# Pinning TensorE's instructions to program order in a two-model, single-core forward pass

## The chip, the cores and the metric

The kernel runs on one core of one Trainium2 chip. The metric is the device time of one execution in microseconds (us). Engine names are those of the profile: PE is TensorE's matrix multiply and PEld its weight load, DVE is VectorE, ACT is ScalarE, POOL is GpSimd, SP is SyncE, which issues the DMAs. Each engine works through a queue of its own, in the order in which the instructions stand there, and the queues wait for each other through semaphores.

## The reference, cut to what matters

Two blocks follow each other on a sequence of 256 positions of width 1024. All data is float32.

```python
def first_block(x, p, ...):                     # D = 1024, S = 256
    for i in range(4):                          # mixers: conv, S5 scan, RWKV7, conv
        y = mixer_i(x, ...)
        r = DN_ALPHA * x + y
        r = r + (p[i] @ ple_proj[i]) * sigmoid(r @ ple_gate[i])
        x = layer_norm(r, ln_g[i], ln_b[i])
    return x

def rwkv7_mixer(x, ...):
    ...
    w_log = -softplus(-(w0 + tanh(xw @ w1) @ w2)) - 0.5      # low-rank: 1024 -> 64 -> 1024
    a = sigmoid(a0 + (xa @ a1) @ a2)
    kk = kk / max(norm(kk), 1e-12)                            # per head of 64
    ...                                                       # recurrence over 256 positions, 16 heads

def half_ffn(h, g, shift, scale, gate, w1, w3, w2):           # 1024 -> 2816 -> 1024
    hm = rms_norm(h, g) * (1 + scale) + shift
    return h + 0.5 * gate * ((silu(hm @ w1) * (hm @ w3)) @ w2)

def second_block(x, c, ctx, c_ctx, ...):
    for l in range(2):
        mod_x, mod_c = silu(c) @ ada_w[l] + ada_b[l], silu(c_ctx) @ ada_w[l] + ada_b[l]
        x, ctx = half_ffn(x, ...), half_ffn(ctx, ...)
        hx, hc = modulated rms_norm of x and of ctx
        y_x, y_c = mixer_ab(hx, hc, ...) if l == 0 else mixer_cd(hx, hc, ...)
        x = x + mod_x[5] * y_x
        x = half_ffn(x, ...)
        if l == 0:
            ctx = half_ffn(ctx + mod_c[5] * y_c, ...)
    return x
```

`mixer_ab` is softmax attention with two kinds of heads, 8 and 8, whose queries and keys get an rms norm per head and a rotation; the tokens attend to 512 keys, their own and those of the context. `mixer_cd` has 8 heads of a chunked gated recurrence and 8 of attention in a window.

## The kernel before

**Matmuls.** Activations stand with their features on the 128 partitions, in 8 chunks of 128 features by 256 positions. A linear layer goes through tiles of weights of 128 by 1024 (8 chunks of 128 by 128). A tile `w` is brought in by a DMA on SP's queue (`get`, L590 to 605), copied into `whi` in the format fp32r by ScalarE (L601), and the rest `wlo` is formed by VectorE (L602). The activations have two halves of the same kind, so that a chunk takes three matmuls into one PSUM bank (`mm3`): hi by whi, lo by whi, hi by wlo. A tile of 8 chunks is thus 24 matmuls of 256 columns. There are four buffers each of `w`, `whi` and `wlo`, and eight PSUM banks: three for `ps_mm`, one for `ps_st`, two each for `ps_ca` and `ps_cb` (`BANKS`).

**Two orders.** The program is written by a planner while it is built. `weave` steps through two generators, the stream of the context (names with 1, as `h1_hi`) and that of the tokens (names with 0, as `d0_hi`), with a model of time of its own: a stream that yields is resumed when its operands should be ready. `par` does the same inside a stage with two or three chains, one for a head or a tile of heads. That gives out a program order for each engine. The tile framework's scheduler then orders each engine's instructions anew by its own estimate of when operands are ready; an instruction wrapped in `keep_in_program_order` can't be moved ahead of the engine's instruction before it, nor that one behind it. Before the change only a few ScalarE instructions are wrapped (table loads and the like).

**Places that the prediction speaks of.**

- `norm_mod` (entry of an FFN): sums of squares through `bsum` into `ps_st`, the root, and then for each of the eight chunks a product `tc` on VectorE, `h_hi` on ScalarE and `h_lo` on VectorE. `ffn` takes its tiles from there.
- `head_norm` (attention heads): the square `ta` of a head's values, `bsum` with a matrix of means (`second`) into a bank, `rsqrt`, and the scaling. `bsum` takes the bank `ps_st`, or a `ps_mm` where its model says that it is free earlier.
- `soft` and `attend` (softmax): scores into `ps_ca`, the maximum and the exponential, `p` times its reciprocal sum on VectorE (`p<-p,sm`), then transposes of `p` into `ps_cb` through `TensorE.transpose` (L437), and the product of the transposed `pt` with the values.
- `rates` and `heads` (RWKV): `rates` multiplies the low-rank vector by three slices of a weight, one after the other through the single bank `ps_st`, each read by a tanh on ScalarE. `heads` then works on two heads of 64 in one chain; its products of 64 by 64 go to `ps_ca` and `ps_cb`. Three chains run at a time.
- A side stream computes the modulation (`in_ada`) on VectorE alone (`junk`, L1379).

Every matmul goes through `TensorE.matmul` (L433), whose helper records the line for all of them, so that places are told apart by tiles.

Of the kernel before, what the change touches and what calls it, by code (L numbers as in the profile page):

```python
# [314 lines left out]
def free_size(ap):  # L315
    n = 1
    for d in ap.shape[1:]:
        n *= d
    return n
# [88 lines left out]
class TensorE:  # L408
# [14 lines left out]
    def matmul(self, out, lhsT, rhs, start, stop, share=1):  # L423

        n, m = free_size(rhs), out.ap[0][1]
        if rhs.dtype == F32R:
            dur = n / 2400.0
        elif m > 64 or share > 1:
            dur = max(n, 128) / 600.0 / share
        else:  # L430
            dur = 0.06 + max(n, 32) / (1200.0 if m > 32 else 2400.0)
        self.count(dur + 0.002, out, [lhsT, rhs])
        self.t.matmul(out, lhsT=lhsT, rhs=rhs, start=start, stop=stop)  # L433

    def transpose(self, out, in_, ident):
        self.count(0.11, out, [in_])
        self.t.transpose(out, in_, ident)  # L437


class Net:  # L440
# [1532 lines left out]
```

## Time and profile before

| | us |
|---|---|
| median of three runs | 2889.77 |
| lowest and highest of these | 2887.61 and 2893.28 |
| the profiled execution | 2890.76 |
| span in its trace | 2889.0 |
| busy: PE / PEld / DVE / ACT / POOL | 2749.4 / 2604.6 / 2134.0 / 1606.4 / 14.8 |
| mean granted TensorE clock, share of full | 0.977 |

The profile comes from one execution. Busy times are sums over all instructions of an engine; the idle time in brackets behind a group of instructions is what its engine stood still just before it, with what ended that. [...] A group such as "x3" in the order in time is that many instructions in a row of one shape with one set of operands.

### The profile page before, as it was taken

Reading aid. Unit: us, or ns where it says so; the run is one execution under the profiler, and the core shown is the slowest. Engines: PE = TensorE matmul, PEld = TensorE weight load, DVE = VectorE, ACT = ScalarE, POOL = GpSimd, SP = SyncE. Lnnn points to the kernel's source line nnn. Section 1 sums busy time; section 2 is a strip of 40 time slices with the busy share of each in tenths; the row PEclk is TensorE's granted clock in tenths of the full one; section 3 lists DMA queues with packets and bytes.
Section 4 is the critical chain, followed back from the end, with each engine's and each line's share of the span. In section 5 each row is a group of like instructions: output and inputs, shape, how many; then the busy total and the mean of one; then the engine's idle time right before and its main releaser. Section 6 shows DMA issues by size and latency. Waiting matters only on the chain.

```text
span 2889.0 us, 58552 instructions
## 1 busy us (share of the span) xinstructions
PE 2749.4 (95%) x23798; PEld 2604.6 (90%) x23798; DVE 2134.0 (74%) x3953; ACT 1606.4 (56%) x2976; POOL 14.8 (1%) x41
## 2 busy tenths in 40 slices
PE   8978799899999998999999999999999999999999
PEld 8967799778998998998999978999999999996999
DVE  8877777666688788899789887777855556676655
ACT  5455555766555465877666766445422234466443
POOL 0000000000000000000000000000000000000000
PEclk9989799999999999999999999999999999999999
DMA  7743355201586665666576644666543433222554
GB/s 270 238 165 110 108 167 175 82 17 40 163 269 226 220 197 167 209 215 203 182 226 195 199 130 155 203 225 194 180 142 125 139 117 103 89 82 65 161 182 139
DMA packets 132751, 467.53 MB, mean 162 GB/s; under 512 B 14720, under 2 KB 19072, under 8 KB 131840
## 3 DMA queue, kind: packets, MB, share of 16 engines
q1 hardware_dynamic: 132480, 463.78, 50.0%
q8 instruction: 187, 3.06, 0.4%
q14 instruction: 84, 0.69, 0.1%
HBM read 462.67 MB, written 1.05 MB: 161 GB/s over the span
## 4 chain that ended last, share of the span: by engine, by line
PE 72%; DVE 12%; DMA 7%; ACT 6%; issue 3%; SPq 0%; ACTq 0%; DVEq 0%
PE ps_mm L433 62%; PE ps_ca L433 5%; DMA w<-in_ada_dram 5%; DVE wlo L602 3%; PE ps_cb L433 2%; DVE junk L1379 2%; PE ps_st L433 2%; DVE ssm_m L403 2%; ACT whi L601 2%; DVE tc L403 1%; PE ps_cb L437 1%; ACT rw_b L403 1%; ACT L403 1%; ACT tc L403 1%; DMA w<-in_ab_in_dram 1%
## 5 line engine op out<-in xcount | busy, mean ns | idle before, releaser
L601 ACT ACTIVATE whi<-w 128x1024 fp32r<-128x1024 f32 (+1 forms) x687 | 715.9, 1043 | 740.2 <-PE ps_mm L433 488.1
L602 DVE TENSOR_TENSOR wlo<-w,whi 128x1024 fp32r<-128x1024 f32 (+1 forms) x687 | 825.6, 1203 | 239.2 <-ACT whi L601 236.8
L433 PE MATMUL ps_mm<-h_hi,whi 128*128 128x256 f32 x3024 | 873.1, 290 | 17.1 <-ACT h_hi L403 12.4
L433 PE MATMUL ps_mm<-h_hi,wlo 128*128 128x256 f32 x3024 | 859.5, 285 | 9.5 <-DVE wlo L602 9.5
L433 PE MATMUL ps_mm<-h_lo,whi 128*128 128x256 f32 x3024 | 856.5, 284 | 0.6 <-DVE h_lo L403 0.5
L433 PEld LDWEIGHTS ps_mm<-h_hi,whi 128*128 128x128 f32 x3024 | 573.6, 190 | 25.8 <-ACT h_hi L403 15.1
L433 PEld LDWEIGHTS ps_mm<-h_hi,wlo 128*128 128x128 f32 x3024 | 573.3, 190 | 12.2 <-DVE wlo L602 11.5
L433 PEld LDWEIGHTS ps_mm<-h_lo,whi 128*128 128x128 f32 x3024 | 577.5, 191 | 5.2 <-DVE h_lo L403 1.9
L1379 DVE SCALAR_TENSOR_TENSOR junk<-w,cond 128x1024 bf16<-128x1024 f32 x288 | 351.7, 1221 | 145.0 <-DMA w<-in_ada_dram 144.1
L433 PE MATMUL ps_mm<-d_hi,whi 128*128 128x256 f32 x1232 | 355.7, 289 | 4.1 <-DVE ctx L403 3.0
L433 PE MATMUL ps_mm<-d_hi,wlo 128*128 128x256 f32 x1232 | 350.4, 285 | 1.5 <-DVE wlo L602 1.5
L433 PE MATMUL ps_mm<-d_lo,whi 128*128 128x256 f32 x1232 | 349.2, 283 | 0.4 <-DVE d_lo L403 0.4
L433 PEld LDWEIGHTS ps_mm<-d_hi,whi 128*128 128x128 f32 x1232 | 232.3, 189 | 8.7 <-issue 5.7
L433 PEld LDWEIGHTS ps_mm<-d_lo,whi 128*128 128x128 f32 x1232 | 234.0, 190 | 3.4 <-issue 1.2
L433 PEld LDWEIGHTS ps_mm<-d_hi,wlo 128*128 128x128 f32 x1232 | 232.1, 189 | 2.8 <-DVE wlo L602 2.0
L403 DVE TENSOR_TENSOR td<-td,ps_mm 128x256 f32<-128x256 f32 x154 | 64.4, 418 | 70.0 <-PE ps_mm L433 68.9
L403 ACT ACTIVATE d_hi<-td 128x256 fp32r<-128x256 f32 x154 | 63.0, 409 | 89.5 <-DVE td L403 88.7
L403 ACT ACT_TABLE_LOAD x78 | 100.1, 1283 | 2.1 <-PEq L1964 0.7
L433 PE MATMUL ps_mm<-x_hi,whi 128*128 128x256 f32 x256 | 73.5, 287 | 12.0 <-ACT whi L601 12.0
L403 ACT ACTIVATE tc<-tc 128x256 f32<-128x256 f32 x182 | 75.1, 413 | 5.6 <-DVE tc L403 2.6
L433 PE MATMUL ps_mm<-xs_hi,whi 128*128 128x256 f32 x256 | 73.4, 288 | 4.8 <-ACT xs_hi L403 4.4
L403 ACT ACTIVATE td<-ps_mm 128x256 f32<-128x256 f32 x154 | 57.4, 374 | 32.9 <-PE ps_mm L433 32.3
(467 smaller groups left out, 5270.5 us busy)
## 6 DMA issues: line engine op xcount, KB each, us to landing
w<-in_ffn_in_dram SPq DMA_DIRECT2D x268, 512.0 KB, 4.2
w<-in_ada_dram SPq DMA_DIRECT2D x168, 512.0 KB, 4.3
w<-in_ffn_out_dram SPq DMA_DIRECT2D x96, 512.0 KB, 4.1
w<-in_conv_in_dram SPq DMA_DIRECT2D x64, 512.0 KB, 4.7
w<-in_ffn_out_dram SPq DMA_DIRECT2D x48, 384.0 KB, 3.1
w<-in_ab_in_dram SPq DMA_DIRECT2D x34, 512.0 KB, 4.4
w<-in_ple_gate_dram SPq DMA_DIRECT2D x32, 512.0 KB, 4.5
w<-in_conv_out_dram SPq DMA_DIRECT2D x16, 512.0 KB, 5.2
```

What stands on the lines that cost most here:

```text
L403: return f(**kw)
L433: self.t.matmul(out, lhsT=lhsT, rhs=rhs, start=start, stop=stop)
L437: self.t.transpose(out, in_, ident)
L601: nc.scalar.activation(out=hi[:, :n], in_=w[:, :n], func=AF.Copy)
L602: nc.vector.tensor_tensor(out=lo[:, :n], in0=w[:, :n], in1=hi[:, :n].bitcast(F32), op=ALU.subtract)
L1379: nc.vector.scalar_tensor_tensor(out=self.junk, in0=w, scalar=1.0, in1=cb[:, s], op0=ALU.mult, op1=ALU.mult, accum_out=m[:, t, s:s + 1])
```

## The change

Both calls that issue a TensorE instruction, in `matmul` and in `transpose`, are wrapped, so that TensorE's queue holds them in the order in which the planner gave them out.

```diff
@@ class TensorE
         self.count(dur + 0.002, out, [lhsT, rhs])
-        self.t.matmul(out, lhsT=lhsT, rhs=rhs, start=start, stop=stop)
+        self.net.tc.keep_in_program_order(self.t.matmul(out, lhsT=lhsT, rhs=rhs, start=start, stop=stop))
 
     def transpose(self, out, in_, ident):
         self.count(0.11, out, [in_])
-        self.t.transpose(out, in_, ident)
+        self.net.tc.keep_in_program_order(self.t.transpose(out, in_, ident))
```

Instructions and their shapes stay the same on all engines. The scheduler still orders the other engines; since it sees another TensorE, 1,056 of VectorE's instructions and some 550 of ScalarE's change place too, most by a few places, and 6 on SP by one. In the rows below, numbers behind a name tell one buffer's use from another.

TensorE before, context FFN (`h1`) beside the tokens' head norms, at the end of a tile:

```order
L433 MATMUL ps_mm_14727<-h1_hi_13309,wlo_14723 128x256
L433 MATMUL ps_mm_14727<-h1_hi_13309,whi_14722 128x256
L433 MATMUL ps_mm_14727<-h1_lo_13310,whi_14722 128x256
L433 MATMUL ps_st_14707<-ta_14661,second_12479 128x256
L433 MATMUL ps_mm_14727<-h1_hi_13309,wlo_14723 128x256
L433 MATMUL ps_mm_14773<-d0_hi_13218,whi_14768 128x256
L433 MATMUL ps_mm_14773<-d0_lo_13219,whi_14768 128x256
L433 MATMUL ps_mm_14773<-d0_hi_13218,wlo_14769 128x256
```

and in the changed program, where the same sum of squares (`ps_st_14707`) stands:

```order
L433 MATMUL ps_mm_14679<-h1_lo_13310,whi_14674 128x256
L433 MATMUL ps_mm_14679<-h1_hi_13309,wlo_14675 128x256
L433 MATMUL ps_st_14707<-ta_14661,second_12479 128x256
L433 MATMUL ps_mm_14727<-h1_hi_13309,whi_14722 128x256
L433 MATMUL ps_mm_14727<-h1_lo_13310,whi_14722 128x256
L433 MATMUL ps_mm_14727<-h1_hi_13309,wlo_14723 128x256
L433 MATMUL ps_mm_14727<-h1_hi_13309,whi_14722 128x256
```

The sum of squares stood inside the tile `ps_mm_14727`, behind 23 of its 24 matmuls; it now stands ahead of that tile.

TensorE before, at the entry of the last FFN (`h0_hi` and `h0_lo` come chunk by chunk, the three banks belong to three weight tiles):

```order
L433 MATMUL ps_st_31405<-squares_31164,cs_base_155 128x256 x2
L433 MATMUL ps_mm_31457<-h0_hi_31415,whi_31452 128x256
L433 MATMUL ps_mm_31490<-h0_hi_31415,whi_31485 128x256
L433 MATMUL ps_mm_31524<-h0_hi_31415,whi_31519 128x256
L433 MATMUL ps_mm_31457<-h0_lo_31416,whi_31452 128x256
L433 MATMUL ps_mm_31457<-h0_hi_31415,wlo_31453 128x256
L433 MATMUL ps_mm_31457<-h0_hi_31415,whi_31452 128x256
L433 MATMUL ps_mm_31490<-h0_lo_31416,whi_31485 128x256
L433 MATMUL ps_mm_31457<-h0_lo_31416,whi_31452 128x256
```

and in the changed program:

```order
L433 MATMUL ps_st_31405<-squares_31164,cs_base_155 128x256 x2
L433 MATMUL ps_mm_31457<-h0_hi_31415,whi_31452 128x256
L433 MATMUL ps_mm_31457<-h0_lo_31416,whi_31452 128x256
L433 MATMUL ps_mm_31457<-h0_hi_31415,wlo_31453 128x256
L433 MATMUL ps_mm_31457<-h0_hi_31415,whi_31452 128x256
L433 MATMUL ps_mm_31457<-h0_lo_31416,whi_31452 128x256
L433 MATMUL ps_mm_31457<-h0_hi_31415,wlo_31453 128x256
```

The three tiles were worked on side by side; now the first is finished ahead of the second, chunk by chunk.

TensorE before, in the tokens' attention beside the context's FFN (`ps_ca` are scores, `ps_cb` transposes of `p`, `d1` is the FFN):

```order
L433 MATMUL ps_mm_19998<-d1_lo_17152,whi_19993 128x256
L433 MATMUL ps_ca_19972<-kava_12481,qa_17666 128x512
L433 MATMUL ps_ca_19982<-kava_12481,qa_17666 128x512
L433 MATMUL ps_mm_19998<-d1_hi_17151,wlo_19994 128x256
L433 MATMUL ps_mm_19998<-d1_hi_17151,whi_19993 128x256
L433 MATMUL ps_mm_19998<-d1_lo_17152,whi_19993 128x256
L433 MATMUL ps_mm_19998<-d1_hi_17151,wlo_19994 128x256
L437 MATMUL ps_cb_19960<-cs_base_155,p_19902 128x128 x4
L433 MATMUL ps_mm_19998<-d1_hi_17151,whi_19993 128x256
```

and in the changed program:

```order
L433 MATMUL ps_mm_19930<-d1_hi_17151,wlo_19926 128x256
L437 MATMUL ps_cb_19960<-cs_base_155,p_19902 128x128 x4
L437 MATMUL ps_cb_19966<-cs_base_155,p_19902 128x128 x4
L433 MATMUL ps_ca_19972<-kava_12481,qa_17666 128x512
L433 MATMUL ps_ca_19982<-kava_12481,qa_17666 128x512
L433 MATMUL ps_mm_19998<-d1_hi_17151,whi_19993 128x256
```

The scores and the tile `ps_mm_19998` stood ahead of the transposes; now the transposes of both heads come first, behind the end of the tile `ps_mm_19930`.

## Rows read from the trace of the kernel before

**Rows 1.** The page: busy time by engine; the chain that ended last, by engine.

```profile
PE 2749.4 (95%) x23798; PEld 2604.6 (90%) x23798; DVE 2134.0 (74%) x3953; ACT 1606.4 (56%) x2976; POOL 14.8 (1%) x41
...
PE 72%; DVE 12%; DMA 7%; ACT 6%; issue 3%; SPq 0%; ACTq 0%; DVEq 0%
```

**Rows 2.** Busy by stage: from:to, length, PE, PEld, DVE, ACT, POOL; clock; DMA.

```profile
526.00:600.00 74.00, 61.85 (x1022) 50.31 (x1020) 42.92 (x105) 53.35 (x134) 1.10 (x1) 0.93 0.10 30
...
1180.00:1350.00 170.00, 165.08 (x1261) 155.62 (x1260) 153.51 (x321) 137.10 (x258) 0.00 (x0) 1.00 0.64 205
1480.00:1660.00 180.00, 176.47 (x1348) 169.66 (x1348) 163.47 (x301) 130.68 (x215) 0.00 (x0) 1.00 0.62 197
1660.00:1770.00 110.00, 108.84 (x713) 80.77 (x711) 87.58 (x201) 76.94 (x145) 0.00 (x0) 1.00 0.41 129
```

**Rows 3.** Order in time, last FFN's entry: start, length, operation [idle before <-releaser].

```profile
2689.61 1.01 PE L433 MATMUL ps_mm<-h_hi,whi 128*128 128x256 f32 x3 [3.44 <-ACT h_hi L403]
...
2694.05 0.41 PE L433 MATMUL ps_mm<-h_hi,whi 128*128 128x256 f32 x1
2694.26 0.60 PE L433 MATMUL ps_mm<-h_lo,whi 128*128 128x256 f32 x2
...
2695.16 0.89 DVE L403 SCALAR_TENSOR_TENSOR h_lo<-tc,mod,h_hi 128x256 fp32r<-128x256 f32 x2 [0.18 <-ACT h_hi L403]
...
2696.85 0.28 PE L433 MATMUL ps_mm<-h_lo,whi 128*128 128x256 f32 x1
2696.97 0.28 PE L433 MATMUL ps_mm<-h_hi,wlo 128*128 128x256 f32 x1
```

**Rows 4.** Busy by stretch, at the same entry.

```profile
2687.90:2694.70 6.80, 5.09 (x24) 5.09 (x25) 6.19 (x16) 2.81 (x7) 0.00 (x0) 0.50 0.19 70
2694.70:2700.00 5.30, 5.30 (x46) 5.30 (x46) 1.59 (x4) 2.33 (x4) 0.00 (x0) 1.00 0.00 0
```

**Rows 5.** Order in time, context FFN beside the tokens' head norms.

```profile
1244.69 0.28 PE L433 MATMUL ps_mm<-h_hi,wlo 128*128 128x256 f32 x1
...
1248.37 0.42 DVE L403 SCALAR_TENSOR_TENSOR tc<-ps_st,tc 128x256 f32<-128x256 f32 x1
...
1248.84 0.70 PE L433 MATMUL ps_st<-ta,second 128*128 128x256 f32 x2 [1.11 <-DVE tc L403]
1249.19 0.47 PE L433 MATMUL ps_mm<-h_hi,wlo 128*128 128x256 f32 x1
...
1251.70 0.42 DVE L403 SCALAR_TENSOR_TENSOR tc<-ps_st,tc 128x256 f32<-128x256 f32 x1
...
1252.36 0.59 PE L433 MATMUL ps_st<-ta,second 128*128 128x256 f32 x2
```

**Rows 6.** Order in time, the tokens' attention beside the context's FFN.

```profile
1662.99 0.28 PE L433 MATMUL ps_mm<-d_hi,whi 128*128 128x256 f32 x1
...
1664.30 1.88 PE L433 MATMUL ps_ca<-kava,qa 128*128 128x512 f32 x4
...
1665.93 0.48 DVE L403 TENSOR_SCALAR p<-p,sm 128x512 f32<-128x512 f32 x1
...
1666.98 0.48 DVE L403 TENSOR_SCALAR p<-p,sm 128x512 f32<-128x512 f32 x1
```

**Rows 7.** Order in time, TensorE alone, start of the RWKV heads.

```profile
526.71 0.59 PE L433 MATMUL ps_mm<-rw_b,cs_base 128*128 128x256 f32 x2
...
535.41 1.13 PE L433 MATMUL ps_st<-rwkv_c,ta 128*128 128x256 f32 x4
...
540.36 1.58 PE L433 MATMUL ps_ca<-rw_a 128*64 128x64 f32 x22 [2.19 <-DVE rw_a L403]
...
548.83 1.48 PE L433 MATMUL ps_cb<-rw_a 128*64 128x64 f32 x18 [3.48 <-DVE rw_a L403]
```

**Rows 8.** Order in time, TensorE alone, heads of two weight tiles.

```profile
1114.50 0.55 PE L433 MATMUL ps_mm<-d_hi,whi 128*128 128x256 f32 x1 [3.04 <-DVE ctx L403]
...
1151.34 0.38 PE L433 MATMUL ps_mm<-h_hi,whi 128*128 128x256 f32 x1 [2.03 <-ACT whi L601]
```

## The prediction, made before the changed kernel was run

> **What bounds the kernel now.** I read the page's busy table first, then its chain of waits, then busy times by stage, then the order in time at the places where the built programs differ. TensorE is busy for 2749.4 of 2889.0 us [rows 1], so at most 139.6 us of its idle time could go, and the chain that ended last lies 72% on TensorE [rows 1]. The reader is to see that this is no stage-by-stage pipeline with slack on TensorE: whatever makes TensorE stand still longer moves the end, unless a later standstill becomes shorter by as much. By stage, VectorE is close behind it: 153.51 of 170 us at 1180 to 1350 and 163.47 of 180 us at 1480 to 1660, against 87.58 of 110 us at 1660 to 1770 [rows 2]. The RWKV start (526 to 600) is the loosest stretch, with 61.85 of 74 us busy [rows 2].
>
> **What the change does to the work.** No instruction is added or removed and none changes its shape. TensorE's stream has 21,145 matmuls and transposes in both programs; 2,976 of them change place, all inside 102 short stretches, between which the two orders are the same. Inside a stretch the old order steps past an instruction whose operand is late and does something else; the new order stands at it. So the cost of a stretch is the wait at the late operand, less what the old order itself waited there. Matmul time is conserved: a 256-column matmul starts 0.12 us after the one before at the full clock (2696.85 to 2696.97) and 0.21 us at the half clock (2694.05 to 2694.26) [rows 3].
>
> For every one of the 102 stretches I took the moment at which each late operand landed in the trace (the end of the ACT or DVE row that writes it), let TensorE start where it started before, walked the new order at the spacings of the rows, and noted how much later the stretch ends. These sums assume that stretches don't affect each other and that the clock is full; one example of each kind follows, with what I keep of its sum.
>
> Stage entries (10 stretches, 28.7 us so counted). A normalisation hands its eight chunks h_hi and h_lo to the next linear layer one after another. At the last FFN, TensorE starts at 2689.61 when the first h_hi is there; the last h_lo lands at 2695.16 + 0.89 = 2696.05 [rows 3]. Before, three weight tiles are worked on at once as chunks arrive: 24 matmuls by 2694.7 at clock 0.50, then 48 more at 0.12 us, to about 2700.4 [rows 4]. In program order the first tile alone has matmuls whose operands are there; its last two can't start before 2696.05, and 48 of the other two tiles remain: 2696.2 + 5.8 = 2702.0, so 1.6 us later, where the full-clock sum said 3.5. Half of the entries stand at the half clock like this one, the others nearer to their full sum: I take 18, with 9 and 29 as bounds.
>
> Head norms (24 stretches, 27.9 us). A head's sum of squares goes into the one ps_st bank, which is free when DVE has read the head before. At 1248.37 + 0.42 = 1248.79 DVE does so, and ps_st starts at 1248.84 [rows 5]. Program order has it right behind the matmul at 1244.69 [rows 5]: a wait of about 4.0 us, where 1.11 was waited before; 23 matmuls that ran meanwhile are still to do, 23 x 0.12 = 2.8 us lost. The next ps_st needs the DVE step of 1251.70 + 0.42 = 1252.12 [rows 5]; behind the first loss TensorE gets there at 1249.2 + 24 x 0.12 = 1252.1 and waits for nothing, though counted alone it cost 2.7. So a pair costs 2.8 and not 5.5. Such neighbours, and a VectorE that catches up while TensorE stands, leave 16 of 27.9; bounds 8 and 28.
>
> Softmax transposes (24 stretches, 41.7 us). Program order puts the transposes of two heads ahead of the next two score matmuls and of a whole FFN tile. TensorE is there at 1662.99; the two p are ready at 1665.93 + 0.48 = 1666.41 and 1666.98 + 0.48 = 1667.46 [rows 6]: 3.4 us, and about 0.6 more behind the first four transposes. Before, none was waited: the scores (1664.30) and 24 FFN matmuls filled it [rows 6]. The scores now start some 4 us later, and with them the next softmax. Part of p's lateness is queueing on VectorE, which is worked off during the wait: I take 29; bounds 14 and 42.
>
> RWKV. Six low-rank products go through the one ps_st bank, three at once at the start. Before, the first head's norm (526.71) and some 5 us of other matmuls ran in between; the third product is at 535.41 [rows 7]. In program order the norm stands behind it, about 9.8 us later, and everything of the first head with it; but TensorE idled 2.19 us before 540.36 and 3.48 before 548.83 [rows 7] waiting for the vector work that this delays, and that work is also held by later queues. Between 0 (the three heads' vector work, not the norm, sets the pace) and 9.8 I take 5, the middle, since ACT and DVE have to do the same work either way. Of the 28 later stretches, 16.1 so counted, I keep 13; bounds 6 and 16.
>
> Others (15 stretches, 2.6 us): a late wlo now holds TensorE instead of the first two matmuls of the next tile, 0.24 us each, and one stretch gets 2.7 us shorter (below). I take 2.
>
> The ACT and DVE queues are reordered too, since their scheduler sees the pinned TensorE, by up to some 30 places; the DMA queue hardly. No row prices that: I keep it at 0, with the bounds of the vector-bound kinds holding it.
>
> Sum: 18 + 16 + 29 + 5 + 13 + 2 = 83 us on the profiled execution's 2890.8: 2973.8. That execution lies 1.0 above the median of 2889.8, so 2973.
>
> [...] The order in the queue matters only if a waiting matmul holds those behind it. In the trace it does: at 1248.84 ps_st had let TensorE idle 1.11 us while the next matmul (1249.19) belonged to a tile of which 23 matmuls had run, so its operands were there [rows 5]. [...]
>
> **Rivals.** (a) The waits are repaid: with TensorE standing, DVE gets through the weight splits earlier and every later vector step is ready sooner. For it: VectorE is busy 90% and 91% in two of the attention stages [rows 2], and the pair above. Against it: at the entries and at the RWKV start nothing else is left to work off. Only those would stay, 18 + 5 less some: about 2908. 12 in 100.
>
> (b) Nothing is repaid and the clock falls. Counted alone the kinds give 117, the RWKV start up to 10. A wait of 3.44 us had the clock at 0.50 until 2694.7 [rows 3, 4]; 24 matmuls there took 5.1 us instead of 2.9, 2.2 lost. Some 15 new waits of over 2 us could each do so, 33 us. Together 2890.8 + 160, near 3050; half of the clock loss, as likely, gives 3030. 20 in 100.
>
> (c) Faster: the old order looked ahead wrongly. It let TensorE stand at the head of the next tile, for a bank (3.04 us at 1114.50) or for its weights (2.03 us at 1151.34) [rows 8], while the present tile was nearly ready. Program order takes these away, 5.1 us with the two shown and up to 9 with smaller ones. It decides if the vector work keeps ahead of TensorE nearly everywhere, so that the other kinds cost less than this: 2881. The softmax rows speak against it, since p is 3.4 us late with VectorE full. 5 in 100.
>
> **How the numbers follow.** The forecast, 2973, has 62 in 100, with its own range from the lower bounds (9 + 8 + 14 + 0 + 6 = 37, so 2927) to the middle of (b) at 3015. Rivals: (a) 12, (b) 20, (c) 5, queue that reorders 1. For 8 in 10 I leave out (c), the reordering queue, the lower part of (a) and the top of (b): 2910 to 3030. A measurement of this kernel can tell about 0.2%, 5.8 us, from no change. Faster by more than that is (c) but for its weaker half: 0.04. Within it: the rest of (c), the reordering queue and the very end of (a): 0.04. Slower: 0.92.
>
> **What would show it.** TensorE's busy time should stay near 2749 us while its idle time grows from 139.6 to some 220. At the last FFN's entry the matmuls should run through one weight tile and stand for each pair of chunks; in the token attention the transposes should carry idle times of 2 to 4 us, ended by DVE's p, and the scores stand behind them; in the RWKV start three ps_st products should follow each other with nothing between. It would be wrong if the idle time ended by p and tc stays where it was although the order moved (a), if the granted clock shows many more stretches at half (b), or if ps_mm waits at tile heads vanish with no others in their place (c).

## The result, and the profile of the changed kernel

The changed kernel takes 3005.1 us (median of four, 3001.8 to 3009.3) against 2890.4 for the kernel before on the same chip: 1.0401 times as long, 95% interval 1.0389 to 1.0414. The prediction was 2973 with a range of 2910 to 3030. It lies within the range; the loss is 114.7 us where 83 were forecast.

The page's busy times answer to [rows 1], with the span and the mean granted clock, a share of full speed (0.977 before):

```profile
PE 2780.8 (93%) x23798; PEld 2623.6 (87%) x23798; DVE 2146.0 (71%) x3953; ACT 1611.7 (54%) x2976; POOL 14.8 (0%) x41
...
PE 14%; DVE 1%; ACT 1%; issue 0%; ACTq 0%
```

```profile
core 0: 3005.2 us, clock 0.963
```

TensorE's idle time is 3005.2 - 2780.8 = 224.4 us, 84.8 more than before; the prediction said "some 220". But its busy time, which was to stay near 2749, rose by 31.4 us with the same 23,798 instructions: 84.8 + 31.4 = 116.2, the whole difference of the spans. The chain of waits can't be held against that of before, since it was followed back over 16% of the span only.

The same stages by busy time, cut at the same instructions as [rows 2]:

```profile
526.00:608.20 82.20, 63.65 (x1018) 51.07 (x1018) 43.69 (x106) 54.42 (x134) 1.10 (x1) 0.85 0.09 27
1211.60:1393.40 181.80, 170.26 (x1253) 158.65 (x1254) 155.61 (x325) 136.34 (x258) 0.00 (x0) 0.97 0.60 192
1523.20:1723.60 200.40, 183.24 (x1348) 176.10 (x1348) 166.63 (x304) 132.35 (x215) 0.00 (x0) 0.96 0.57 180
1723.60:1853.40 129.80, 111.43 (x713) 83.43 (x712) 88.98 (x198) 76.50 (x145) 0.00 (x0) 0.96 0.33 105
```

The reader is to see two things in each line: it is longer by more than TensorE's busy time grew, which is idle time, and the granted clock, 1.00 in three of these stages before and 0.93 in the first, is now 0.85 to 0.97.

TensorE's instructions between the 102 stretches stand in the same order in both traces, so that one can read at every stretch how far the changed kernel has fallen behind. Grouped as in the prediction (one stretch was put to another group than ahead), with the growth between stretches given to the stretch that follows (all in us; the column of idle time counts inside the stretches alone):

| kind | stretches | kept in the sum | fell behind | of it idle inside |
|---|---|---|---|---|
| stage entries | 10 | 18 | 20.8 | 10.3 |
| head norms | 25 | 16 | 20.1 | 15.7 |
| softmax transposes | 23 | 29 | 44.4 | 30.3 |
| RWKV start | 1 | 5 | 8.0 | 6.2 |
| RWKV later | 28 | 13 | 16.1 | 17.7 |
| others | 15 | 2 | 7.1 | 6.8 |
| sum | 102 | 83 | 116.5 | 87.0 |

With idle time alone the sum was nearly met, but not kind by kind: the entries stood 8 us less than was kept for them, the RWKV mixer's later places and the others 5 us more each.

### The profile page after: what moved, and what is told of

The parts are those of the page before. It is cut to its first block, busy times and chain, and to the rows that moved or that the text cites. A ratio compares the mean times of both kernels' runs of the same rounds, so it can differ in the third digit from the quotient of the medians.

```text
span 3005.2 us, 58587 instructions
## 1 busy us (share of the span) xinstructions
PE 2780.8 (93%) x23798; PEld 2623.6 (87%) x23798; DVE 2146.0 (71%) x3953; ACT 1611.7 (54%) x2976; POOL 14.8 (0%) x41
## 5 line engine op out<-in xcount | busy, mean ns | idle before, releaser
L433 PE MATMUL ps_mm<-h_hi,whi 128*128 128x256 f32 x3024 | 887.6, 294 | 17.5 <-ACT h_hi L403 17.0
L433 PE MATMUL ps_mm<-h_lo,whi 128*128 128x256 f32 x3024 | 866.9, 287 | 8.5 <-DVE h_lo L403 7.6
L433 PEld LDWEIGHTS ps_mm<-h_hi,wlo 128*128 128x128 f32 x3024 | 581.2, 192 | 7.7 <-DVE wlo L602 7.7
L437 PE MATMUL ps_cb<-cs_base,p 128*128 128x128 f32 x256 | 44.1, 297 | 42.4 <-DVE p L403 33.9
L437 PEld LDWEIGHTS ps_cb<-cs_base,p 128*128 128x128 f32 x256 | 29.7, 149 | 57.5 <-issue 24.4
```

Of the source, the lines that this page charges most:

```text
L433: self.net.tc.keep_in_program_order(self.t.matmul(out, lhsT=lhsT, rhs=rhs, start=start, stop=stop))
L437: self.net.tc.keep_in_program_order(self.t.transpose(out, in_, ident))
```

## Experiments

**One kind of place at a time.** Four kernels pin TensorE only over ranges of its program order; in each the places of that kind stand as in the changed kernel and nearly all others as before. In the order of the table below 24, 26, 12 and 29 of the 102 stretches have the changed kernel's order, 88 different ones in all; the other 14, which fell 5.5 us behind under the whole change, are pinned in none. With the head norms pinned, 11 short stretches of the softmax stages behind came out in an order that neither program has.

```diff
 class TensorE:
+    def pin(self, ins):
+        if any(a <= self.n < b for a, b in PINNED):
+            self.net.tc.keep_in_program_order(ins)
+        self.n += 1
...
-        self.t.matmul(out, lhsT=lhsT, rhs=rhs, start=start, stop=stop)
+        self.pin(self.t.matmul(out, lhsT=lhsT, rhs=rhs, start=start, stop=stop))
```

> TensorE is pinned only in the softmax stages (context attention, tokens' attention, the last attention in windows); 23 of the changed places stand as in the changed kernel, all others but one as before. Theory: what the full change cost in these stages belongs to these places alone; between the same instructions the two traces grow apart there by 38.6 us inside the places and 5.8 between them, so 2890 + 44 = 2934 (2929 to 2940). The prediction's own term was 29 (2919). Rival (the loss comes from the whole program's new order on VectorE and ScalarE, or the stages pay each other back): well off 2934, near 2890 or above 2950.

> TensorE is pinned only in the stages of the attention heads' norms. Theory: 21.0 us inside the places less 1.0 between them, so 2890 + 20 = 2910 (2905 to 2916); the prediction's term was 16. But at the tokens' heads a later softmax may take the loss up, since the order of the attention behind is free again. Rival as for the softmax alone: near 2890, or above 2925.

> TensorE is pinned only at the ten stage entries. Theory: 24.5 us inside the places less 3.7 between, so 2890 + 21 = 2911 (2905 to 2917), of which idle time only 10 and the rest a lower clock; the prediction's term was 18, with no clock in it. Rival: the clock at the entries fell because of waits elsewhere; then only the idle time stays and the kernel takes 2900.

> TensorE is pinned only in the RWKV mixer (from the first products of rates to the end of its heads). Theory: 8.0 us at the start and 19.1 less 3.1 behind it, so 2890 + 24 = 2914 (2908 to 2920), nearly all of it idle time; the prediction's term was 18. Rival as above: near 2890.

| pinned | median us | against 2888.3 | ratio, 95% interval | idle | busy |
|---|---|---|---|---|---|
| softmax | 2937.5 | +49.2 | 1.0167 (1.0152 to 1.0182) | +33.0 | +15.0 |
| head norms | 2906.0 | +17.7 | 1.0059 (1.0042 to 1.0076) | +12.2 | +5.8 |
| entries | 2912.9 | +24.6 | 1.0080 (1.0065 to 1.0095) | +5.5 | +18.2 |
| RWKV | 2911.0 | +22.8 | 1.0079 (1.0064 to 1.0094) | +23.3 | -3.4 |

The last two columns come from the busy line of each page and the span, against 2749.4 of 2889.0 in [rows 1]: spans of 2937.0, 2907.0, 2912.7 and 2908.9 us, in the order of the table with

```profile
PE 2764.4 (94%) x23798; PEld 2611.8 (89%) x23798; DVE 2139.5 (73%) x3953; ACT 1609.4 (55%) x2976; POOL 14.8 (1%) x41
```

```profile
PE 2755.2 (95%) x23798; PEld 2610.2 (90%) x23798; DVE 2135.0 (73%) x3953; ACT 1603.9 (55%) x2976; POOL 14.8 (1%) x41
```

```profile
PE 2767.6 (95%) x23798; PEld 2616.2 (90%) x23798; DVE 2134.9 (73%) x3953; ACT 1607.9 (55%) x2976; POOL 14.8 (1%) x41
```

```profile
PE 2746.0 (94%) x23798; PEld 2600.7 (89%) x23798; DVE 2134.8 (73%) x3953; ACT 1605.8 (55%) x2976; POOL 14.8 (1%) x41
```

All four times lie in the ranges of the theory; of the entries' loss 5.5 us are idle time, where 10 were expected. The four losses add up to 114.3 us, each known to some 4 us, and the loss of the whole change is 114.7: the stages don't pay each other back, and the new order on VectorE and ScalarE elsewhere is not what costs. Inside a pinned stage the order of VectorE and ScalarE changes with TensorE's, and no run parts the two. The last columns show where each kind loses: the entries mostly in longer busy time (18.2 us, 5.5 of idle time), the RWKV mixer in idle time alone, the softmax stages in both.

Which instruction waits is read from the groups of instructions, whose last field is the idle time before the group and what ended it: the transposes of `p`, and the rotation of a head (`ps_ca<-tb,second`), before:

```profile
L437 PE MATMUL ps_cb<-cs_base,p 128*128 128x128 f32 x256 | 40.7, 278 | 3.9 <-DVE p L403 2.1 <-DVE sm L403 1.3
L433 PE MATMUL ps_ca<-tb,second 128*128 128x256 f32 x42 | 13.6, 406 | 2.5 <-DVE tb L403 2.1
L433 PE MATMUL ps_st<-ta,second 128*128 128x256 f32 x40 | 12.5, 393 | 2.0 <-DVE tc L403 1.9
```

in the changed kernel:

```profile
L437 PE MATMUL ps_cb<-cs_base,p 128*128 128x128 f32 x256 | 44.1, 297 | 42.4 <-DVE p L403 33.9 <-DVE sm L403 5.8 <-ACT d_hi L403 1.3
L433 PE MATMUL ps_ca<-tb,second 128*128 128x256 f32 x42 | 13.9, 414 | 14.3 <-DVE tb L403 14.3
L433 PE MATMUL ps_st<-ta,second 128*128 128x256 f32 x40 | 12.4, 392 | 3.9 <-DVE tc L403 3.6 <-ACT ta L403 0.2
```

with the softmax stages alone pinned, and with the head norms alone:

```profile
L445 PE MATMUL ps_cb<-cs_base,p 128*128 128x128 f32 x256 | 45.0, 300 | 42.9 <-DVE p L403 35.4 <-DVE sm L403 4.0 <-ACT whi L609 1.5
L441 PE MATMUL ps_ca<-tb,second 128*128 128x256 f32 x42 | 13.6, 406 | 2.4 <-DVE tb L403 2.0
```

```profile
L441 PE MATMUL ps_ca<-tb,second 128*128 128x256 f32 x42 | 13.8, 410 | 16.3 <-DVE tb L403 16.3
```

The transposes' wait, 3.9 us before, is 42.4 under the whole change and 42.9 when only these stages are pinned.

**Is it the standing that takes the clock down?** Eight matmuls that nobody reads were put behind the last sum of squares at three entries, in the changed kernel (`a_warm`) and in the one before (`b_warm`); `a_trickle` adds two small ones behind each of the first seven chunks of the tokens' first weight tile. Each of these matmuls stands as two rows in the trace (eight of them take the 74 rows of the stretch below to 90).

```diff
+    def warm(self, lhsT, rhs, n):
+        ps = self.psum["ca"].tile([128, 512], F32, name="ps_ca")
+        for k in range(n):
+            i = self.T.t.matmul(ps[:, :S], lhsT=lhsT, rhs=rhs, start=k == 0, stop=k == n - 1)
+            self.tc.keep_in_program_order(i)
...
         ms = self.bsum(self.c("mean"), lambda k: sq[:, k * (NCH - 1)], 2)
+        if g == 2 and s == 0:
+            self.warm(self.c("mean"), sq[:, 0], 8)
```

> The changed kernel with eight more matmuls (128x256, operands long there, result read by nobody) behind the last sum of squares at three stage entries: the entry of the last conv mixer, and the entries of the tokens' second FFN in both layers. They run where TensorE stood for 4.4, 4.6 and 3.4 us with nothing else to do. In the changed kernel some 28.5 us of TensorE's work behind these three entries ran at the half clock. Theory (the stand-still is what brings the clock down, and that is the part that the sum left out): half of 28.5 comes back, 3005 - 14 = 2991 (2987 to 2998). Rival (the clock falls for another reason, or comes back only with the stage): 3005 to 3008, as work was added.

> The kernel before with the same eight matmuls at the same three entries. There 14.5 us of work behind them ran at the half clock. Theory: half of it comes back, 2890 - 7 = 2883 (2880 to 2886). Rival: 2890 to 2893.

> As a_warm, and at the two FFN entries two more small matmuls (128x128, operands long there, result read by nobody) behind each of the first seven chunks of the tokens' first weight tile, 28 in all: where program order makes TensorE stand for the next pair of chunks. In a_warm the first wait was covered, yet the clock fell again 1.8 to 3.7 us after the first chunk and stayed low for 6.8 us at each of the two entries. Theory (it is the standing between the chunks, which only program order brings, that takes the clock down there): the granted clock stays at 1.00 over both entries, and from the last sum of squares to the end of the first three tiles they take some 16.5 us instead of 19; the kernel takes 2997 to 3001, a_warm 3002. Rival (the clock doesn't hang on these waits): still a stretch at 0.50 at each, and 3002 to 3006.

Measured: `a_warm` 3002.4 us, 1.0380 (1.0357 to 1.0402); `a_trickle` 3001.0, 1.0390 (1.0374 to 1.0406); `b_warm` 2887.5, 0.9992 (0.9983 to 1.0001). The times alone settle nothing: none can be told from the kernel that it was made from. `a_warm` and `b_warm` lie between the ranges of their theory and their rival, `a_trickle` on the border. The stretch from the last sum of squares to the end of the first three weight tiles of the last FFN does, in busy times (the figure behind POOL's is the granted clock). Before, and with the eight matmuls:

```profile
2685.50:2700.70 15.20, 11.76 (x74) 11.18 (x74) 9.64 (x20) 7.14 (x13) 0.00 (x0) 0.78 0.17 57
```

```profile
2683.60:2697.10 13.50, 13.46 (x90) 12.28 (x90) 9.73 (x20) 7.33 (x14) 0.00 (x0) 1.00 0.16 60
```

In the changed kernel, then with the eight, and with the 14 small ones besides:

```profile
2798.70:2817.50 18.80, 15.20 (x76) 13.31 (x77) 11.78 (x23) 9.12 (x17) 0.00 (x0) 0.73 0.23 74
```

```profile
2800.30:2819.20 18.90, 17.65 (x92) 15.39 (x93) 11.72 (x23) 9.14 (x17) 0.00 (x0) 0.82 0.21 72
```

```profile
2792.00:2809.30 17.30, 17.16 (x120) 15.61 (x121) 11.70 (x23) 9.16 (x17) 0.00 (x0) 1.00 0.24 76
```

Before, covering the one wait is enough: the clock is 1.00 instead of 0.78 and the stretch is 1.7 us shorter with more work in it (16.6 to 14.2 at the same place of the layer before). Of what these stretches won, the whole span kept 3.8 us (2889.0 to 2885.2) and the median 2.2, where 7 were expected. Under program order it is not: with the wait covered the clock still fell, later (0.82 over the stretch, 0.73 without), and nothing was won (18.9 us for 18.8). Only when the waits between the chunks were filled too did it stay at 1.00, at both entries, and the stretch fell from 18.8 to 17.3 (19.5 to 18.0 at the other), where 16.5 was expected. With the standing between chunks, which program order brings, the clock was 0.82 over each of these entries, and without it 1.00: the theory on the clock holds there, seen at two entries in one profiled execution of each kernel. The times that it gave for `a_warm` were too low because two kinds of wait were taken for one, and because a higher clock wins little while chunks still come: some 1.86 us lie between two pairs of them at 0.50 as at 1.00. In the changed kernel (clock 0.50) the first matmuls of two pairs of chunks start here:

```profile
2804.40 0.41 PE L433 MATMUL ps_mm<-h_hi,wlo 128*128 128x256 f32 x1
2804.72 0.58 PE L433 MATMUL ps_mm<-h_hi,whi 128*128 128x256 f32 x1
...
2806.57 0.58 PE L433 MATMUL ps_mm<-h_hi,whi 128*128 128x256 f32 x1
```

and in `a_warm`, before the clock falls, here:

```profile
2806.27 0.38 PE L433 MATMUL ps_mm<-h_hi,whi 128*128 128x256 f32 x1 [0.43 <-ACT h_hi L403]
...
2808.13 0.40 PE L433 MATMUL ps_mm<-h_hi,whi 128*128 128x256 f32 x1 [0.43 <-ACT h_hi L403]
```

At either clock a pair follows the last after 1.85 or 1.86 us, the pace at which ScalarE hands over `h_hi` in the changed kernel (2804.16, 2806.01, 2807.87). At 1.00 the wait shows as 0.43 us of idle time. At 0.50 the longer row of the matmul before (2804.40 + 0.41) reaches over the next start, and the same wait counts as busy. So longer busy time at 0.50 is in part clock and in part hidden standing.

**Later transposes.** The planner was told that `p` comes later, so that more of the other stream's work stands ahead of the transposes.

```diff
-        yield 3.5 if bias is None else 4.3
+        yield Until(self.end + 2.0)
```

> The changed kernel, but the planner lets each softmax's transposes come 2.0 us later by its own time than its model says that p is ready. Between a score matmul and its transposes TensorE then has 30 to 60 other instructions in the tokens' attention, where the changed kernel has 9 to 29 and the one before 30 to 40; in the last attention (in windows) there is hardly other work, and the distance stays short. Theory (the order stands at p too early, and the work that would cover it is there): the context's and the tokens' softmax losses, 28 us between them, mostly go, the last attention's 18 stay: 3005 - 22 = 2983 (2977 to 2990). Rival (VectorE is full there, so p moves back with the rest, and a wait is only put off): 3000 to 3008.

It took 3037.0 us, 1.0501 (1.0481 to 1.0522), slower than the change itself and outside both ranges. The groups of instructions show what changed:

```profile
L437 PE MATMUL ps_cb<-cs_base,p 128*128 128x128 f32 x256 | 41.0, 286 | 26.2 <-DVE p L403 22.3 <-DVE sm L403 1.6 <-DVE nb L403 0.9
L433 PE MATMUL ps_ca<-tb,second 128*128 128x256 f32 x42 | 17.1, 495 | 28.6 <-DVE tb L403 25.0 <-DVE tc L403 3.5
L403 ACT ACT_TABLE_LOAD x104 | 133.4, 1283 | 2.6 <-PEq L1964 0.7
```

The wait at the transposes went down from 42.4 to 26.2, and 15.8 of what is left lies in the last attention, which has no other stream: that much is as expected. But at the heads' rotations TensorE waits 28.6 instead of 14.3 (the likely reading is that the FFN work that now stands ahead of the transposes is missing there), and in the new interleaving ScalarE loads its tables 104 times at line 403 instead of 78, 33 us more of it. Neither theory had that. Of the 31.0 us by which the span is longer than the changed kernel's (3036.2 for 3005.2), 17.9 are idle time of TensorE and 13.1 busy time (2793.9 for 2780.8); which of the causes they go back to was not measured.

**The low-rank products of the RWKV mixer.** `a_rates` gives the second and third product a bank of their own; `a_rates2` does so while the planner books them as before, so that its order is the changed kernel's; `a_rates3` issues the later five one by one.

```diff
-                ps = self.ps("st")
+                ps = self.ps("mm" if f in (1, 2) else "st")
```

> The changed kernel, but of the three low-rank products at the RWKV start the second and third go to banks of ps_mm, so that they needn't wait for ScalarE to read the first out of the one ps_st. Theory (the products in a row through one bank hold the first head's norm): most of the start's 8.0 us goes, 3005 - 6 = 2999 (2996 to 3002). Rival (the heads' vector work sets the pace there and the norm is not what it waits for): 3003 to 3007.

```diff
-                ps = self.ps("st")
+                b = "mm" if f in (1, 2) else "st"
+                ps = self.model.alloc(self.psum[b].tile([128, 512], F32, name="ps_" + b), "st", 1)
```

> As a_rates, but the planner still books the three products under the one bank, so that its order is the changed kernel's everywhere, and only the banks of two products differ. In a_rates the stages up to the end of the RWKV mixer took 11.6 us less than in the changed kernel and the attention behind, in another order, 20 us more. Theory (one bank held the first head's norm; the loss behind belongs to the other order): 3005 - 9 = 2996 (2992 to 2999). Rival (a_rates gained from another order within the mixer, not from the bank): 3003 to 3007.

```diff
-            if f % 3 == 2:
-                rates(range(f + 1, min(f + 4, NCH)))
...
             V.scalar_tensor_tensor(out=bv, in0=bv, scalar=64.0, in1=bon, op0=MUL, op1=MUL)
+            if f + 3 < NCH:
+                rates((f + 3,))
```

> The changed kernel, but the low-rank products of the later heads, which rates issues in threes (4th to 6th, then 7th and 8th), are issued one by one, each late in the head three before its own. In the changed kernel TensorE stands 10.6 us in front of these five (4.26, 3.02, 0.95, 2.36 behind the first of each batch), ended by ScalarE, and 4.9 in front of the first three; before the change all eight together cost 1.2. The planner's order of the attention far behind shifts too, so that this run is read in its stage: from the first low-rank product to the mean of that layer's normalisation, 340.5 us before, 368.4 in the changed kernel, 368.7 with other banks for the first three (a_rates2). Theory (program order makes TensorE stand until ScalarE has read the product before out of the bank, and that waits for a head's vector work): the waits in front of these five go and the stage takes 358 us (355 to 361). Rival (the heads' vector work sets the pace, and TensorE waits for it a little later instead): 366 to 370.

They took 3016.0, 3008.5 and 3030.3 us: 1.0427 (1.0404 to 1.0449), 1.0410 (1.0391 to 1.0428) and 1.0485 (1.0467 to 1.0502). The first fits neither theory. The second lies 1.5 us above the rival's range and the range lies within its interval; the third fits the rival in its stage; its span is 23 us longer than the changed kernel's, lost behind that stage, where its order is another. In `a_rates2` the bank did what it should, as the order in time on TensorE shows:

```profile
528.44 0.59 PE L433 MATMUL ps_st<-rwkv_c,ta 128*128 128x256 f32 x2
530.15 0.70 PE L433 MATMUL ps_st<-rwkv_c,ta 128*128 128x256 f32 x2 [1.11 <-ACT rwkv_c L403]
530.68 1.89 PE L433 MATMUL ps_mm<-rwkv_c,ta 128*128 128x256 f32 x8
532.41 0.59 PE L433 MATMUL ps_mm<-rw_b,cs_base 128*128 128x256 f32 x2
...
546.72 2.08 PE L433 MATMUL ps_st<-rwkv_c,ta 128*128 128x256 f32 x4 [7.63 <-ACT rw_a L403]
553.20 2.08 PE L433 MATMUL ps_st<-rwkv_c,ta 128*128 128x256 f32 x4 [4.40 <-ACT rw_a L403]
```

The first head's norm (`ps_mm<-rw_b`) comes 4.0 us behind the first product, not 10.1; yet the next batch of products waits 7.63 and 4.40 where the changed kernel waits 4.26 and 3.02, and the stage takes 368.7 us against 368.4. In `a_rates3` the eight products together still wait 15.7 us (15.5 in the changed kernel, 1.2 before), now in front of the fourth (7.51), and the stage takes 367.7. So neither the one bank at the start nor the batches are what costs. The likely reading is that TensorE, wherever a product stands in a fixed order, waits there for the heads' work on VectorE and ScalarE, and that the old order let the heads' matmuls of the other chains by. No run shows this by itself, and which of that work sets the pace is left open. The first of the three shows a trap besides: its RWKV stage was 11.6 us shorter, but its planner also ordered the attention differently, and that cost 20.

**Faster than both.** What the clock runs taught was used on the kernel before: `b_warm2` covers four more waits.

```diff
+        if (l, g, s) in ((0, 2, 0), (1, 2, 0), (1, 1, 0), (0, 0, 1)):
+            self.warm(self.c("mean"), sq[:, 0], 8)
...
+        if i == 0:
+            self.warm(self.c("mean"), total, 14)
         sq = self.slot(2, [NCH, S], "sq")
```

> As b_warm, with such matmuls at four more places of the kernel before where TensorE stands with nothing else to do: the first layer's normalisation (14 behind the mean, 8 behind the variance), the context's first FFN entry (8) and the norm ahead of the last mixer (8). Behind these some 25 us of work ran at the half clock. Theory (covering a wait keeps the clock up, and the matmuls behind it are on the path): b_warm's stages took 6.8 us less; 3.5 more at the normalisation, 2.8 at the mixer, up to 4 at the FFN entry: 2890 - 13 = 2877 (2872 to 2883). Rival (in these stages VectorE and ScalarE set the end): 2884 to 2890.

2885.5 us, 0.9984 (0.9975 to 0.9992): faster than the kernel before by some 4 us (2889.4 beside it), a third of what was expected, and the lowest median here. That lies in the rival's range, so that waiting for VectorE and ScalarE is not ruled out for most of these stages. The mean granted clock rose from 0.977 to 0.986. Part of the shortfall is plain: the 14 matmuls in the first layer's normalisation were too many and held its variance up, 13.3 us from mean to variance instead of 8.6.

## Why the prediction was right, and where it was not

- **That it loses, and roughly how much idle time**: right. The wait at the late operand, taken from the landing times in the trace of before, gave 80 us more idle time; it was 84.8. That it comes so near is in part luck, since the kinds miss in both directions (table above). No run shows a ground for the queue that reorders (1 in 100): in [rows 5] a ready matmul stood behind a waiting one for 1.11 us, and pinned, the transposes wait 42.4 us instead of 3.9.
- **"The clock is full"**: this is the step that failed. It was set down as an assumption of the sums; the clock's price (33 us) was worked out in rival (b), and there joined with "nothing is repaid". The two came apart: idle time grew about as forecast, and busy time by 31.4 us on top, at a lower clock. The trace's clock records have 34 stretches at 0.50, 222.5 us of the span, where the kernel before has 18 and 132.8 us. They didn't come as (b) had it, by some 15 new waits of over 2 us: TensorE's waits of over 2 us went from 22 to 30, those of over 1 us from 36 to 70. Not all of the 31.4 us is the clock's, since standing is hidden in it (above), and no run divides it for the whole kernel. So it is luck that 83 + 31.4 comes within a microsecond of the loss.
- **Stage entries**: 18 kept, 20.8 and 24.6 measured, but only 5.5 to 10.3 of it idle. At the last FFN the first tile runs through as foreseen (the answer to [rows 3, 4]; order in time, TensorE and the last `h_lo`):

```profile
2802.86 0.39 PE L433 MATMUL ps_mm<-h_hi,whi 128*128 128x256 f32 x1 [3.44 <-ACT h_hi L403]
...
2808.41 0.88 DVE L403 SCALAR_TENSOR_TENSOR h_lo<-tc,mod,h_hi 128x256 fp32r<-128x256 f32 x2 [0.18 <-ACT h_hi L403]
...
2812.96 0.41 PE L433 MATMUL ps_mm<-h_lo,whi 128*128 128x256 f32 x1
2813.17 0.37 PE L433 MATMUL ps_mm<-h_hi,wlo 128*128 128x256 f32 x1
2813.38 0.28 PE L433 MATMUL ps_mm<-h_hi,whi 128*128 128x256 f32 x1
2813.49 0.28 PE L433 MATMUL ps_mm<-h_lo,whi 128*128 128x256 f32 x1
```

  The last chunk is there at 2809.29, but the next tiles run at 0.21 us each until 2813.4 and only then at 0.12. Before, full speed was back at 2694.7, ahead of the last chunk. That makes 3.5 us at this entry where 1.6 was said. The clock's part can be read off: behind the last chunk 19 matmul starts take 4.05 us (2809.33 to 2813.38), at 0.12 us they would take 2.3, so 1.8 us are the clock's, and the order itself cost the 1.6 of the prediction within 0.1.
- **Head norms**: 16 kept, 20.1 and 17.7 measured, but the place was right for the context alone. There the example holds (answer to [rows 5]):

```profile
1279.44 0.70 PE L433 MATMUL ps_st<-ta,second 128*128 128x256 f32 x2 [2.71 <-DVE tc L403]
...
1284.34 0.59 PE L433 MATMUL ps_st<-ta,second 128*128 128x256 f32 x2
```

  2.71 us in front of the first and nothing in front of the second: 3.1 for the pair where 2.8 was said. At the tokens' heads, three quarters of the places, TensorE stands at the rotation `ps_ca<-tb,second` (14.3 us, 2.5 before) for the product on VectorE, not at `ps_st` for its bank (3.9, 2.0 before). The size came out of the replay of all places, the mechanism was read off one of them.
- **Softmax transposes**: the term that was sized worst, 29 for 44.4 (49.2 alone). Its idle time was nearly met, 30.3 us inside the stretches and 33.0 with these stages alone pinned. What is missing is busy time, 15.0 us more of it with these stages alone pinned, and under the whole change the clock in the tokens' attention is 0.96 instead of 1.00. But the idle time came about otherwise than said. The first wait is indeed smaller than said, 1.41 us for 3.4 (answer to [rows 6]):

```profile
1728.11 1.09 PE L437 MATMUL ps_cb<-cs_base,p 128*128 128x128 f32 x8 [1.41 <-DVE p L403]
1729.04 1.88 PE L433 MATMUL ps_ca<-kava,qa 128*128 128x512 f32 x4
...
1734.94 0.63 PE L437 MATMUL ps_cb<-cs_base,p 128*128 128x128 f32 x4 [1.15 <-DVE sm L403]
...
1741.41 0.95 PE L437 MATMUL ps_cb<-cs_base,p 128*128 128x128 f32 x4 [2.25 <-DVE p L403]
```

  But the scores behind it are late by that, so is the next softmax, and TensorE waits again at the pairs that follow (1.15, 2.25). The prediction says so itself ("and with them the next softmax") and gives it no price. That the third which it struck out of 41.7 and these later waits about cancel is luck. In the last attention, which has no other stream beside it, TensorE waits 18.0 of the 42.4 us in front of transposes, 0.2 before.
- **RWKV start**: 5 kept between 0 and 9.8, 8.0 measured; the norm did come 9.7 us later. The account by one bank fell with `a_rates2`. The two waits named against it (2.19 and 3.48 in [rows 7]) are gone in the changed kernel, and others stand in their place, in front of the fourth and fifth product: 4.26 and 3.02.
- **Rival (c)**: the waits of [rows 8] did go or shrink, and were given back at once. The 3.04 us at the bank, and 1.49 behind it in front of `wlo`, became 5.75 in front of `wlo`; the stretch ahead of the 2.03 won 4.05 us, the one that holds it lost 5.03, with waits of 1.78, 0.90, 0.69 and 0.82 in its place. **Rival (a)**, a repayment of nearly everything, finds no support: the four parts add up to the whole, and between the stretches, summed by kind, the changed kernel won back 10 us and lost 6.
- **Slips that change no term**: the low-rank products are eight, not six (the slices of 1024 by 128); half the clock loss in (b) gives 3034, not 3030, and no sum gives its 3015; the built programs move instructions of VectorE by up to 37 places and of ScalarE by up to 63, not some 30.

## What to carry to other kernels

A scheduler's order that looks untidy may be what covers the waits: before pinning an engine, replay the pinned order against the landing times of the trace, and count the queue's followers, too, when the late operand feeds a chain that comes back to the same queue. Price the clock with the new waits and not as a case of its own: where TensorE got its work in drips here, at the two FFN entries, the granted clock was 0.73 and 0.74 (0.78 and 0.79 before), and at the last FFN it was still 0.50 for the 4.1 us of work behind the last chunk. And when a planner's figure is changed to test one wait, compare the instruction order of all other stages first, since the whole plan shifts with it.

## What the runs showed of the hardware

Adding eight matmuls to the kernel before at each of two FFN entries shortened these by 1.7 and 2.4 us, with the granted clock at 1.00 instead of 0.78 and 0.79. Under program order one covered wait wasn't enough: the clock was 0.73 at the last FFN's entry, 0.82 with the wait covered, and 1.00 only when the waits between chunks were filled too. And with the mean granted clock at 0.963 instead of 0.977 the page has 31.4 us more busy time for the same 23,798 rows. That reads like more work and isn't: at the last FFN's entry matmuls of 256 columns started 0.21 us apart at 0.50 and 0.12 at 1.00, and the longer rows (0.41 us for 0.28) cover waits, as the 0.43 us that the trace shows at 1.00 and not at 0.50. What each of the two adds over the whole kernel was not measured.
